# A decoder layer on one core: attention's eight PSUM banks dealt out by use instead of in mixed rings

## The chip, the cores and the metric

The kernel runs on one core of a Trainium2 chip. The metric is the device time of one execution in microseconds (us). The kernel before took 2240.39 us, the median of three runs (2234.24 to 2243.52).

## The reference

One decoder layer on 1040 positions (16 meta tokens and 1024 tokens) of width 1024, in float32:

```python
h = h + 0.5 * rms_norm(swiglu(rms_norm(h, g_ffn1_pre), w_ffn1_in, w_ffn1_out), g_ffn1_post)
u = rms_norm(h, g_mix_pre)
q, k, v, f_logit, c_b, c_c, c_in, gate_a, gate_c = split_cols(u @ w_in)
log_f = jax.nn.log_sigmoid(f_logit + b_forget)
y_attn = forgetting_attention(q, k, v, log_f) @ w_attn_branch   # softmax(q.k/8 + F[t] - F[s], causal) @ v
y_conv = (c_b * short_conv(c_c * c_in, conv_w)) @ w_conv_branch
mixed = (sigmoid(gate_a) * y_attn + sigmoid(gate_c) * y_conv) @ w_out
h = h + rms_norm(mixed, g_mix_post)
h = h + 0.5 * rms_norm(swiglu(rms_norm(h, g_ffn2_pre), w_ffn2_in, w_ffn2_out), g_ffn2_post)
```

Attention has 8 heads of 64 channels; F is the running sum of log_f.

## The kernel before, in words

Every float32 operand of a large product is split into a high and a low part, and a product is three matmuls (`mm3`, L142 to L146): high by high, low by high, high by low. The first feed-forward block, the projections, convolution and attention, the mixing, and the second feed-forward block follow each other. The stage that the change touches lies at about 740 to 1440 us of the span.

That stage goes like this. `values_in` (L728) projects the values of nine token blocks. Four passes (L828) compute the short convolution. Then a loop over 8 heads and 4 query pairs (L992 to L1009) runs attention. For each pair of heads `project_heads` (L901) multiplies out q and k, five pieces named `pqk`: two of q (512 columns each), three of k (264, 264, 512). ScalarE (L913) and VectorE (L914) drain each piece into one of two buffers `ha`, and SyncE copies it by DMA into `q` and `k` (L921, L923), four copies a piece. `softmax` (L925) multiplies scores into PSUM (`sc`, L937), one to three pieces for a query block; VectorE adds the forget bias and takes the minimum (L938), ScalarE the exponential (L942), VectorE the reciprocal and the scaling (L943, L944). `values` (L947) treats the query pair before: it transposes the weights, up to four 128x128 blocks into one bank (`tp`, L966), ScalarE and VectorE split the bank into two halves of a small buffer `hbc` (L139, L140; two places each, taken in turn), and two matmuls per key block (`pv`, L975 with the high half, L977 with the low) add into one output bank of 256 columns. ScalarE copies half of that bank out (L982), VectorE adds the other half (L983), the sum is split (L139, L140), and a DMA on ScalarE's queue stores it to `atd` (L986).

Between these dependent steps stands independent work: `fill_work` (L857) yields 32 gate projections (`pg`, 24 matmuls each) and then 16 products of the convolution branch (`pcb`, 12 matmuls each). Their results go into half pages (`tt`, L754) of a ring of four pages that the outputs of `values` use too, so that a gate result can wait for the store of an old attention output.

The order of the instructions on each engine is not the order of the code: a scheduler (`schedule_with_timeline_sim`) simulates the program with its own costs and takes, on each engine, the earliest instruction of the code that it thinks ready. What the engine gets is a fixed sequence, and an instruction whose input is late holds up everything behind it on its engine. The banks decide in it when a matmul may start: `Turns` (class in the code) deals out bank numbers in rotation, and the next user of a bank waits until the last one's result is read.

Before, `psO` deals banks 0 to 3 in one rotation to the scores and to the outputs, `psA` banks 4 and 5 to all projections and fill products, `psT` banks 6 and 7 to the transposed weights.

Of the kernel before, what the change touches and what calls it, by code (L numbers as in the profile page):

```python
# [49 lines left out]
class Split:  # L50
# [5 lines left out]
    def at(self, *sl):  # L56
        return Split(self.h[sl], self.l[sl])


def f32(ap):  # L60
    return ap.bitcast(F32)
# [6 lines left out]
def hybrid_layer(ctx, tc, x, meta, w_in, b_forget, conv_w, w_attn, w_conv, w_out,  # L68
# [69 lines left out]
    def split_into(h, l, src, eng=None):  # L138
        S.copy(h, src)  # L139
        (eng or V).tensor_sub(l, src, f32(h))  # L140
# [563 lines left out]
    def tH(tag, shape, name):  # L704

        turn[tag] += 1
        t = hbc[:, {"HB": 0, "HC": 2}[tag] + turn[tag] % 2]
        return t.rearrange("p a n -> p (a n)")[:, :shape[0] * shape[1]].rearrange("p (a n) -> p a n", a=shape[0])
# [38 lines left out]
        mix_input(1)  # L747


    psO, psA, psT = Turns(0, 1, 2, 3).bank, Turns(4, 5).bank, Turns(6, 7).bank  # L750
    loc = {"X": Turns(0, 1, 2, 3), "k": Turns(4, 5), "t": Turns(6, 7, 8, 9)}
    half_page = []

    def tt(n, name, dt=F32):  # L754

        if not half_page:
            t = loc["t"].page(name)
            half_page.extend((t[:, W0:W0 + H], t[:, :H]))
        t = half_page.pop()[:, :n]
        return t.bitcast(dt) if dt != F32 else t  # L760
# [185 lines left out]

    def values(h, qp, pr, v):  # L947

        po = psO(f"pv{h}_{qp}")[:, :256]
        first_mm = True  # L950
        vb, vm = v
        for s in range(2):
            V.tensor_copy(pmet[:, s, :META], pr[s][:, :META])
        for g in range(qp + 1, -1, -1):

            blks = [2 * g - 1, 2 * g] if g else [0]
            tp = psT(f"tp{h}_{qp}_{g}")

            at = lambda j, s: slice(256 * j + P * s, 256 * j + P * s + P)
            first_s = {2 * qp + 2: 1}  # L960
            hi = 0
            for j, b in enumerate(blks):
                k0 = META + P * (b - 1)
                for s in range(first_s.get(b, 0), 2):
                    c = at(j, s) if b <= 2 * qp + 1 else at(j, 0)
                    nc.tensor.transpose(tp[:, c], pr[s][:, k0:k0 + P] if b else pmet[:, s], ident)  # L966
                    hi = c.stop
            pth = tH("HB", [2, 256], f"pth{h}_{qp}_{g}").rearrange("p a b -> p (a b)")
            ptl = tH("HC", [2, 256], f"ptl{h}_{qp}_{g}").rearrange("p a b -> p (a b)")
            split_into(pth[:, :hi], ptl[:, :hi], tp[:, :hi])  # L970
            for j, b in enumerate(blks):
                vv = vb[:, b - 1, :] if b else vm
                s = first_s.get(b, 0)
                o, c = po[:, P * s:], slice(256 * j, 256 * j + 256 - P * s)
                mm(o, vv, pth[:, c], start=first_mm, stop=False)  # L975
                first_mm = False
                mm(o, vv, ptl[:, c], start=False, stop=b == 0)  # L977

        i = h % 2
        a, bo = DH * i, DH * (1 - i)  # L980
        os = tt(256, f"os{h}_{qp}")
        S.copy(os[a:a + DH], po[bo:bo + DH])  # L982
        V.tensor_add(os[a:a + DH], po[a:a + DH], os[a:a + DH])  # L983
        oh = tt(512, f"oh{h}_{qp}", F32R).rearrange("p (a b) -> p a b", a=2)
        split_into(oh[a:a + DH, 0], oh[a:a + DH, 1], os[a:a + DH])
        nc.scalar.dma_start(out=atd[:, a:a + DH, h // 2, qp * 256:qp * 256 + 256].rearrange("s p t -> p s t"),  # L986
                            in_=f32(oh[a:a + DH]))
# [4 lines left out]
    for h in range(NH):  # L992
        if h % 2 == 0:
            project_heads(h // 2)
        fb = fbuf[:, h % 2, :L]
        nc.sync.dma_start(out=fb, in_=fd[h:h + 1, :].broadcast_to([P, L]))
        v = (vbuf[:, h % 2], vmet[:, h % 2])
        load(f32(v[0]), vd[h, :, 1:, :])
        load(f32(v[1]), vd[h, :, 0, :])
        for qp in range(3, -1, -1):  # L1000
            pr = [softmax(h, 2 * qp + 1, fb), softmax(h, 2 * qp, fb)][::-1]
            if pend is not None:
                values(*pend)
            pend = (h, qp, pr, v)
            step += 1

            while done < (min(step * 32 // 25, 32) if step <= 25 else min(32 + (step - 25) * 16 // 7, 48)):
                next(fill)
                done += 1  # L1009
    values(*pend)  # L1010
    for _ in fill:
        pass

# [234 lines left out]
```

## Time and profile before

| | |
|---|---|
| profiled execution | 2236.28 us, span 2234.2 us, mean granted TensorE clock 0.978 |
| median of three timed runs | 2240.39 us |
| PE (matmul) busy | 2116.9 us, 95% of the span |
| DVE, ACT, POOL busy | 1434.0, 794.3, 140.5 us |
| chain that ended last | PE 80%, DMA 9%, DVE 7% |

PE is TensorE, DVE VectorE, ACT ScalarE, SP SyncE. A matmul's row gives a modelled length that overlaps the next one's: the distance from start to start, which the chain of waits prints, is what it takes of PE's time. The granted clock is 1.00 at 2.4 GHz and 0.50 at 1.2 GHz.

### The profile page before, as it was taken

To read this page: it belongs to the slowest core of one execution; us is meant where nothing else is said; L and a number is where in the kernel's file an instruction comes from. 1 tells how busy PE (TensorE), PEld (TensorE's weight loads), DVE (VectorE), ACT (ScalarE), POOL (GpSimd) and SP (SyncE) were. 2 spreads that over 40 slices of the span, in tenths; PEclk is the share of its full clock that TensorE was granted. 3 is DMA by queue.
4 is the path that set the end of the run, shared out by engine and by line. 5 is a ranking of instruction groups with operands and counts; after the bars stand their busy time and mean duration, and the time that the engine had idled before them with its cause. 6 is when DMAs were issued, how large, how long until landed. Compare 5 with 4: busy or idle time off the path is not lost.

```text
span 2234.2 us, 29992 instructions
## 1 busy us (share of the span) xinstructions
PE 2116.9 (95%) x11590; PEld 1835.9 (82%) x11590; DVE 1434.0 (64%) x2315; ACT 794.3 (36%) x1291; POOL 140.5 (6%) x181
## 2 busy tenths in 40 slices
PE   5899999999997999999999999899799999999996
PEld 5799999999886998888888787688588888878875
DVE  7976666655868643345454457656886666647788
ACT  6322222234234421134343344334432222224434
POOL 3000000000003200000010000012000000000000
PEclk9899999999999999999999999999899999999998
DMA  4322222368556542343434273833132222278574
GB/s 133 101 90 86 86 73 75 89 227 272 173 162 228 176 138 76 87 117 96 130 111 123 63 231 115 259 132 121 58 120 83 77 81 84 85 247 280 189 222 173
DMA packets 276967, 305.45 MB, mean 137 GB/s; under 512 B 12908, under 2 KB 184760, under 8 KB 276824
## 3 DMA queue, kind: packets, MB, share of 16 engines
q1 hardware_dynamic: 241072, 242.94, 35.8%
q10 hardware_dynamic: 35720, 60.59, 7.8%
q8 instruction: 91, 1.49, 0.3%
q14 instruction: 52, 0.43, 0.1%
q0 software_dynamic: 32, 0.00, 0.0%
HBM read 233.47 MB, written 57.36 MB: 130 GB/s over the span
## 4 chain that ended last, share of the span: by engine, by line
PE 80%; DMA 9%; DVE 7%; issue 2%; ACT 1%; SPq 1%; POOL 0%; ACTq 0%; POOLq 0%; DVEq 0%
PE wP L144 6%; PE wP L145 6%; PE wP L146 6%; PE vP L144 6%; PE vP L145 6%; PE vP L146 6%; PE pg L144 3%; PE pg L146 2%; PE pg L145 2%; PE 2P L145 2%; PE 2P L144 2%; PE 2P L146 2%; PE P L144 2%; PE P L145 2%; PE P L146 2%; DMA arP<-in_w_ffn_out_dram 2%
## 5 line engine op out<-in xcount | busy, mean ns | idle before, releaser
L145 PE MATMUL P<-blP,ahP 128*128 128x264 f32 (+1 forms) x452 | 144.7, 322 | 4.1 <-DVE ms_m0b L186 4.0
L144 PE MATMUL P<-bhP,ahP 128*128 128x264 f32 (+1 forms) x452 | 139.0, 324 | 8.4 <-ACT bhP L139 4.2
L146 PE MATMUL P<-bhP,alP 128*128 128x264 f32 (+1 forms) x452 | 143.8, 321 | 0.0
L145 PE MATMUL 2P<-lb2P,ha2P 128*128 128x512 f32 x264 | 103.8, 393 | 2.4 <-DVE lb2P L140 2.3
L146 PE MATMUL 2P<-hb2P,la2P 128*128 128x512 f32 x264 | 102.9, 391 | 0.0
L144 PE MATMUL 2P<-hb2P,ha2P 128*128 128x512 f32 x264 | 96.3, 394 | 2.8 <-ACT ha2P L139 2.4
L144 PEld LDWEIGHTS P<-bhP,ahP 128*128 128x128 f32 x452 | 85.7, 193 | 15.7 <-ACT bhP L139 5.2
L145 PEld LDWEIGHTS P<-blP,ahP 128*128 128x128 f32 x452 | 86.6, 192 | 10.4 <-DVE blP L140 4.9
L146 PEld LDWEIGHTS P<-bhP,alP 128*128 128x128 f32 x452 | 86.4, 191 | 5.7
L140 DVE TENSOR_TENSOR hbc<-tp,hbc 128x512 fp32r<-128x512 f32 (+2 forms) x112 | 62.8, 572 | 18.4 <-ACT hbc L139 17.3
L139 ACT CAST hbc<-tp 128x512 fp32r<-128x512 f32 (+2 forms) x112 | 52.8, 494 | 58.3 <-PE tp L966 55.6
L930 POOL TENSOR_TENSOR fbuf<-fbuf,rows 128x128 f32<-128x128 f32 x64 | 31.3, 489 | 576.5 <-DVE mn L938 481.9
L942 ACT ACTIVATE p<-p,mn 128x1040 f32<-128x1040 f32 (+3 forms) x64 | 50.6, 790 | 35.5 <-DVE mn L938 30.1
L145 PEld LDWEIGHTS 2P<-lb2P,ha2P 128*128 128x128 f32 x264 | 50.0, 189 | 14.5 <-DVE lb2P L140 4.1
L144 PEld LDWEIGHTS 2P<-hb2P,ha2P 128*128 128x128 f32 x264 | 49.7, 189 | 14.2 <-ACT ha2P L139 2.9
L937 PE MATMUL sc<-k,q 128*128 128x392 f32 (+6 forms) x224 | 54.7, 337 | 5.2 <-DVE mn L938 2.0
L146 PEld LDWEIGHTS 2P<-hb2P,la2P 128*128 128x128 f32 x264 | 49.9, 189 | 10.4
L938 DVE CUSTOM_DVE_ANT_0 p<-sc,fbuf 128x16 f32<-128x16 f32 (+3 forms) x64 | 28.5, 450 | 43.6 <-PE tp L966 30.5
L144 PE MATMUL pg<-um1h,g_h 128*128 128x512 f32 x128 | 51.4, 401 | 1.7 <-ACT oh L864 0.6
L144 PE MATMUL wP<-u1T2h,ws32h 128*128 128x264 f32 x176 | 50.9, 290 | 1.9 <-ACT u1T2h L139 1.2
L146 PE MATMUL wP<-u1T2h,ws32l 128*128 128x264 f32 x176 | 50.6, 289 | 2.0 <-DVE ws32l L140 2.0
L144 PE MATMUL pg<-um0h,g_h 128*128 128x512 f32 x128 | 50.8, 397 | 0.7 <-DVE ha L914 0.7
(795 smaller groups left out, 6914.9 us busy)
## 6 DMA issues: line engine op xcount, KB each, us to landing
arP<-in_w_ffn_out_dram SPq DMA_DIRECT2D x35, 512.0 KB
rb2P<-in_w_ffn_out_dram SPq DMA_DIRECT2D x35, 512.0 KB
ra2P<-g2d SPq DMA_DIRECT2D x30, 512.0 KB
wrb<-in_w_ffn_in_dram SPq DMA_DIRECT2D x22, 512.0 KB
vrb<-in_w_ffn_in_dram SPq DMA_DIRECT2D x22, 512.0 KB
g2d<-vuc ACTq DMA_DIRECT2D x44, 256.0 KB
brP<-g1d SPq DMA_DIRECT2D x20, 528.0 KB
wra<-in_w_ffn_in_dram SPq DMA_DIRECT2D x19, 512.0 KB
```

The lines of the kernel that those rows point to most:

```text
L139: S.copy(h, src)
L140: (eng or V).tensor_sub(l, src, f32(h))
L144: mm(o, a.h, b.h, start=start, stop=False)
L145: mm(o, a.h, b.l, start=False, stop=False)
L146: mm(o, a.l, b.h, start=False, stop=stop)
L930: G.tensor_add(fb[:, nk - P:nk], fb[:, nk - P:nk], mask)
L937: mm(sc[:, :ke - k0], q[:, s, qt * P:qt * P + P], k[:, k0:ke], start=s == 0, stop=s == 1)
L938: V.tensor_tensor_reduce(out=p[:, k0:k1], in0=sc[:, :k1 - k0], in1=fb[:, k0:k1], scale=1.0, scalar=mn[:, j - 1:j] if j else 3e38, op0=ALU. ...
L942: S.activation(p[:, :nk], p[:, :nk], AF.Exp, bias=low, scale=-1.0, accum_out=mn[:, 3:4])
```

## The change

From the convolution to the end of attention the banks are dealt out by use: banks 0 and 1 for scores (and for the last four blocks of `values_in`), 2 and 3 for projections and fill products, 5 to 7 for transposed weights, and bank 4 alone for the outputs of `values`. After attention the three old rotations are set up again.

```diff
-    psO, psA, psT = Turns(0, 1, 2, 3).bank, Turns(4, 5).bank, Turns(6, 7).bank
+    psO, psA, psT, psV = Turns(0, 1).bank, Turns(2, 3).bank, Turns(5, 6, 7).bank, Turns(4).bank
...
     def values(h, qp, pr, v):
 
-        po = psO(f"pv{h}_{qp}")[:, :256]
+        po = psV(f"pv{h}_{qp}")[:, :256]
...
     for _ in fill:
         pass
+
+    psO, psA, psT = Turns(0, 1, 2, 3).bank, Turns(4, 5).bank, Turns(6, 7).bank
```

No operation is added or taken away; PE has the same matmuls. The scheduler puts them in another order in this stage. Three places on PE show it.

First, the outputs of head 7, query pair 2. In the order before, two groups of transposes and their first output matmuls (`tp_2_2`, `tp_2_1`, then `pv_2`) stand back to back:

```order
L977 MATMUL pv_3_12601<-hbc,vmet 128x256
L966 MATMUL tp_2_2_12740<-ident,p_4_12587 128x128
L966 MATMUL tp_2_2_12740<-ident,p_5_12573 128x128
L966 MATMUL tp_2_2_12740<-ident,p_4_12587 128x128
L966 MATMUL tp_2_2_12740<-ident,p_5_12573 128x128
L966 MATMUL tp_2_1_12751<-ident,p_4_12587 128x128
L966 MATMUL tp_2_1_12751<-ident,p_5_12573 128x128
L966 MATMUL tp_2_1_12751<-ident,p_4_12587 128x128
L966 MATMUL tp_2_1_12751<-ident,p_5_12573 128x128
L975 MATMUL pv_2_12727<-hbc,vbuf 128x256
```

In the order now a score piece and two more groups stand between `tp_2_1` and `pv_2`, and `tp_2_2` has moved ahead of a whole fill product:

```order
L966 MATMUL tp_2_1_12751<-ident,p_4_12587 128x128
L966 MATMUL tp_2_1_12751<-ident,p_5_12573 128x128
L966 MATMUL tp_2_1_12751<-ident,p_4_12587 128x128
L966 MATMUL tp_2_1_12751<-ident,p_5_12573 128x128
L937 MATMUL sc_0_0_12831<-k_1_11818,q_1_11817 128x256 x2
L966 MATMUL tp_2_0_12762<-ident,pmet 128x128 x2
L966 MATMUL tp_1_2_12841<-ident,p_2_12717 128x128
L966 MATMUL tp_1_2_12841<-ident,p_3_12703 128x128 x2
L975 MATMUL pv_2_12727<-hbc,vbuf 128x256
```

So the transposes have moved away from the matmuls that read them.

Second, on PE, the scores of head 5 right behind the outputs of head 4 (`pv_0`). Before, six score pieces crowd behind one output, each in a bank that an output or a score has just left:

```order
L975 MATMUL pv_0_11412<-hbc,vmet 128x256
L937 MATMUL sc_6_0_11401<-k_1_10782,q_1_10781 128x456 x2
L977 MATMUL pv_0_11412<-hbc,vmet 128x256
L937 MATMUL sc_5_1_11472<-k_1_10782,q_1_10781 128x392 x2
L937 MATMUL sc_4_1_11486<-k_1_10782,q_1_10781 128x328 x2
L937 MATMUL sc_4_0_11482<-k_1_10782,q_1_10781 128x328 x2
L937 MATMUL sc_3_0_11610<-k_1_10782,q_1_10781 128x264 x2
L937 MATMUL sc_3_1_11614<-k_1_10782,q_1_10781 128x264 x2
L144 MATMUL pg_512_11691<-um1h_7280,g_h 128x512
```

Now there are output matmuls between the first pieces, and a gate projection follows the third:

```order
L937 MATMUL sc_6_0_11401<-k_1_10782,q_1_10781 128x456 x2
L977 MATMUL pv_1_11300<-hbc,vbuf 128x256
L975 MATMUL pv_1_11300<-hbc,vbuf 128x256
L977 MATMUL pv_1_11300<-hbc,vbuf 128x256
L966 MATMUL tp_0_0_11425<-ident,pmet 128x128 x2
L975 MATMUL pv_1_11300<-hbc,vmet 128x256
L937 MATMUL sc_6_1_11405<-k_1_10782,q_1_10781 128x456 x2
L977 MATMUL pv_1_11300<-hbc,vmet 128x256
L937 MATMUL sc_5_0_11468<-k_1_10782,q_1_10781 128x392 x2
L144 MATMUL pg_0_11580<-um0h_6271,g_h 128x512
```

The crowd has been spread over the gate projections.

Third, on PE, the first scores of the last pair of heads, which read k fresh from its DMA. Before, after `sc_7_0` come five transposes and a long run of gate matmuls (`sc_7_1` stands 35 of them later):

```order
L937 MATMUL sc_7_0_11980<-k_0_11816,q_0_11815 128x16 x2
L966 MATMUL tp_0_1_12012<-ident,p_0_11729 128x128
L966 MATMUL tp_0_1_12012<-ident,p_1_11719 128x128 x2
L966 MATMUL tp_0_0_12022<-ident,pmet 128x128 x2
L144 MATMUL pg_0_12035<-um0h_6271,g_h 128x512
```

Now only six output matmuls and two gate matmuls stand between:

```order
L937 MATMUL sc_7_0_11980<-k_0_11816,q_0_11815 128x16 x2
L975 MATMUL pv_0_12009<-hbc,vbuf 128x256
L977 MATMUL pv_0_12009<-hbc,vbuf 128x256
L975 MATMUL pv_0_12009<-hbc,vbuf 128x128
L977 MATMUL pv_0_12009<-hbc,vbuf 128x128
L975 MATMUL pv_0_12009<-hbc,vmet 128x256
L977 MATMUL pv_0_12009<-hbc,vmet 128x256
L144 MATMUL pg_0_12035<-um0h_6271,g_h 128x512
L145 MATMUL pg_0_12035<-um0l_6273,g_h 128x512
L937 MATMUL sc_7_1_11984<-k_0_11816,q_0_11815 128x512 x2
```

The second score has moved towards the copies of k.

## Rows read from the trace of the kernel before

**Rows 1.** Busy time by stretch: stretch, length, busy of engines, clock, DMA, GB/s.

```profile
966.00:1078.00 112.00, 109.81 (x599) 93.78 (x597) 57.41 (x158) 47.54 (x98) 7.50 (x16) 1.00 0.38 104
1078.00:1192.00 114.00, 110.65 (x601) 94.21 (x600) 58.94 (x160) 46.87 (x98) 8.72 (x16) 1.00 0.43 117
1192.00:1309.00 117.00, 111.13 (x592) 94.26 (x593) 57.41 (x158) 45.49 (x96) 7.51 (x16) 0.99 0.34 96
1309.00:1410.00 101.00, 92.80 (x496) 77.71 (x494) 69.91 (x187) 46.54 (x101) 6.67 (x14) 0.98 0.57 177
1410.00:1425.00 15.00, 8.82 (x27) 6.58 (x27) 3.49 (x8) 2.46 (x5) 0.00 (x0) 0.66 0.97 330
```

**Rows 2.** Who PE waited for, 966 to 1425: total us, times, longest us.

```profile
PE pab L145 <- DMA ab1l<-atd: 3.4, 1, 3.4
PE pv L977 <- DVE hbc L140: 3.3, 7, 0.6
...
PE pqk L144 <- ACT oh L864: 2.1, 1, 2.1
PE pv L975 <- ACT hbc L139: 2.0, 3, 1.1
PE sc L937 <- DVE mn L938: 2.0, 3, 0.8
...
PE sc L937 <- DVE os L983: 1.5, 2, 0.8
PE sc L937 <- DMA k<-ha: 1.4, 2, 1.2
...
PE tp L966 <- DVE hbc L140: 1.0, 1, 1.0
...
PE pg L144 <- ACT oh L864: 0.6, 1, 0.6
PE pg L144 <- ACT gt L864: 0.6, 1, 0.6
PE pqk L144 <- ACT gt L864: 0.6, 1, 0.6
```

**Rows 3.** Chain of waits, two pieces: start us, us from start to start.

```profile
986.34 0.76 PE tp L966 x7
...
1253.20 0.12 PE pv L975
1253.32 0.23 PE pg L146
```

**Rows 4.** Groups by line, splitting of transposed weights: busy us, mean ns, idle before.

```profile
L140 DVE TENSOR_TENSOR hbc<-tp,hbc 128x512 fp32r<-128x512 f32 (+2 forms) x112 | 62.8, 572 | 18.4 <-ACT hbc L139 17.3
L139 ACT CAST hbc<-tp 128x512 fp32r<-128x512 f32 (+2 forms) x112 | 52.8, 494 | 58.3 <-PE tp L966 55.6 <-DVE hbc L140 1.0 <-issue 0.5
```

**Rows 5.** Timeline by engine, 1252 to 1264: start, us, instruction, idle before.

```profile
1257.86 0.65 PE L937 MATMUL sc<-k,q 128*128 128x456 f32 x2 [0.72 <-DVE os L983]
1258.66 0.37 ACT L982 COPY gt<-pv 64x256 f32<-64x256 f32 x1 [0.51 <-PE pv L977]
1259.59 0.41 DVE L983 TENSOR_TENSOR gt<-pv,gt 64x256 f32<-64x256 f32 x1
```

**Rows 6.** Timeline by engine at the first scores, 940 to 975.

```profile
966.37 0.36 PE L937 MATMUL sc<-k,q 128*128 128x16 f32 x2
970.21 1.03 PE L937 MATMUL sc<-k,q 128*128 128x512 f32 x4
966.41 0.43 DVE L914 SCALAR_TENSOR_TENSOR ha<-pqk,ha 128x264 fp32r<-128x264 f32 x1 [7.30 <-ACT ha L913]
```

**Rows 7.** Groups by line: the softmax of one query block.

```profile
L938 DVE CUSTOM_DVE_ANT_0 p<-sc,fbuf,mn 128x512 f32<-128x512 f32 (+4 forms) x48 | 30.7, 640 | 20.8 <-PE sc L937 17.4 <-POOL fbuf L930 2.5 <-issue 0.3
L942 ACT ACTIVATE p<-p,mn 128x1040 f32<-128x1040 f32 (+3 forms) x64 | 50.6, 790 | 35.5 <-DVE mn L938 30.1 <-DVE mn L943 4.1
L944 DVE TENSOR_SCALAR p<-p,mn 128x1040 f32<-128x1040 f32 (+3 forms) x64 | 35.8, 562 | 1.8
```

## The prediction

> **What bounds the kernel now.** I read the busy time by stretch first. In the four stretches that hold attention, 966 to 1410 us, PE is busy for all but 2.2, 3.4, 5.9 and 8.2 us (length less busy time), 19.6 us in all [rows 1]. So PE sets the pace, the change takes no matmul from it, and what it can win is what PE loses between matmuls in these 444 us. The list of waits comes second and says what these 19.6 us are [rows 2]. I sort them by what the banks can do to them.
>
> A. Transposed weights: `pv` and `tp` waiting for the split into `hbc`: 3.3 + 2.0 + 1.0 = 6.3 us, 11 times.
> B. Scores waiting for a bank that another score or an output still holds (`sc` for `mn` L938 and `os` L983): 2.0 + 1.5 = 3.5 us, 5 times.
> C. Projections waiting for a gate result (`oh` and `gt`, L864): 2.1 + 0.6 + 0.6 + 0.6 = 3.9 us, 4 times. ScalarE can't write it, because the half page is still to be stored from an older attention output.
> D. Scores waiting for k: 1.4 us.
>
> What is left of the 19.6 are waits for `ha` and for loads, which I leave as they are. Behind attention PE loses another 6.2 us of 15 (15.00 less 8.82) before the attention branch's product, since that waits for a load of the stored outputs [rows 1, 2].
>
> The third view is the chain of waits, for what a matmul takes from start to start: 0.23 us for 512 columns, 0.12 for 256, 0.76/7 = 0.11 for a transpose [rows 3]. With these I price the work that stands on PE between two instructions in the order of before and of the change. It is no forecast of a time, only how much cover each wait has, and it is how the terms below are scaled: a measured wait, times cover missing now over cover missing before.
>
> **The change part by part.**
>
> Three banks for transposed weights (A). A transpose's result is ready for the high matmul after ScalarE's 0.494 us, for the low one after VectorE's 0.572 more [rows 4]; with about 0.1 for handing over I ask 0.6 and 1.2 us of cover. The order of before falls below 1.2 us to the high matmul in 22 of the 112 groups, the order now in 2. That is not all the cover that counts: `hbc` still has only two places, so a split also waits until the output matmuls two groups back have read theirs. With both conditions the missing cover sums to 5.7 us before and 1.7 now. 6.3 x 1.7/5.7 = 1.9, so A wins 4.4 us. The bounds: 6.3 if all of it goes, 0 if the two places of `hbc` decide.
>
> Two banks for scores, one for outputs (B). A score's bank is read in 0.64 us on VectorE [rows 7]. An output's bank is read by ScalarE from 1258.66 and by VectorE until 1259.59 + 0.41 = 1260.00, which is 1.34 us [rows 5]. Asking 0.85 and 1.3, the order before lacks cover at 13 handovers, 7.0 us together; the order now at 8, 3.7 us together. The crowd of six score pieces of head 5, one of whose waits is the 0.72 us in [rows 5], is spread out. 3.5 x 3.7/7.0 = 1.8: B wins 1.7 us, between 3.5 and a loss that is the first rival below.
>
> Gate results (C). Places where a projection comes less than 5 us of cover behind the last output matmul whose store frees its half page: six before, three now. I take off a third: 1.3 us, between 0 and 3.9.
>
> Copies of k (D), a new cost. With fewer banks in the mixed ring, the scheduler brings the second score of a head pair (`sc_7_1`) forward. In the second, third and fourth pair it now stands 1.9, 2.1 and 1.2 us of work behind the first score. It reads keys 16 to 527, whose second piece is drained at about the moment of the first score: at the first pair the drain starts at 966.41, the first score at 966.37, and the second score starts at 970.21 without a wait [rows 6]. So the copy arrives no later than 3.8 us after the drain's start, and no earlier than the drain itself (0.43). With 3.8 the three waits sum to 1.9 + 1.7 + 2.6 = 6.2 us, with 0.43 to nothing; I take the upper middle, 3.6, since four DMAs must be issued for each piece. Against that, the first score of the third pair now has some 2 us more cover behind its q, which pays back 1.2 of the 1.4 us of D. Behind the waiting score stand the gate matmuls, so PE stands still for all of it. Net loss 2.4.
>
> Later softmax. Scores come later, so their weights come later before the transposes: the least cover from the last score to the first transpose falls from 4.2 us to 2.2 and 2.3, in two places. The path is 0.64 + 0.79 + 0.56 = 2.0 us at mean sizes [rows 7], plus handing over and what VectorE has in front. I take 1 us at each of the two: loss 2, between 0 and 4.
>
> Clock and restarts. The granted clock is 0.99 over 117 us and 0.98 over 101 [rows 1], which is 1.2 + 2.0 = 3.2 us of work lost; after waits of several us it has fallen towards the half level (0.66 in the last stretch). Fewer waits give back 1 us (0 to 3.2). A row shows a wait only past the modelled end of the matmul before; some 12 fewer waits at the 0.16 us that it so hides (estimate: about 0.28 us of row length against 0.12 from start to start) give 2 more.
>
> What stays. The wait at 1410 stays: it begins with the drain of head 7's second-to-last outputs, and both orders put about 8 us of PE work behind that. Before 966 PE is taken as covered in both orders; 24 matmuls of the first convolution product only move into the end of the mixing block. Price of being wrong there: about 1 us either way. After attention the orders agree, and the shift goes through to the end.
>
> Sum: -4.4 - 1.7 - 1.3 + 2.4 + 2.0 - 1.0 - 2.0 = -6.0 us. The profiled execution took 2236.28, so 2230.3; its time lies 4.1 below the median of the three runs, so for a median I predict 2240.4 - 6.0 = 2234.
>
> **A rule that speaks against it.** The Trainium skill says in "Perfetto Trace Analysis", section "Optimizing Tensor Performance", that independent matmul groups should go round different PSUM banks, so that draining one overlaps the next group's matmuls. The 31 handovers from one output to the next no longer do that. By that rule, with nothing else between, 31 drains of 1.34 us would be added, 42 us, and the sum would come to 2276. The trace of before can't show a ring of one; what it shows is one score waiting 0.72 us for an output's bank [rows 5], and the sum above counts the cover instead. The mechanism is weighed as the first rival.
>
> **Rivals.**
>
> 1. The single output bank (slower). Place: the 31 handovers from one output to the next. For it: the readers of that bank stand in ScalarE's and VectorE's queues behind other work, and everything on PE stands behind the next `pv`. Against it: in the order now only 3 handovers have under 1.3 us of other PE work between. If the drain takes 3 us, the missing cover is 11 us; 4 us, 19; 5 us, 31. With 4 us: -6 + 19 = +13, 2253. It eats the gain from 2.2 us on (5.9 missing there) and costs 0.5% from 3.9. For a drain to be that long the queues would have to be three times as late as in [rows 5].
>
> 2. The waits change place (no change). k's copies cost their upper bound, 6.2 - 1.2 = 5.0, and softmax 4: -4.4 - 1.7 - 1.3 - 3.0 + 9.0 = -1.4 us, 2239. For it: both new costs are bounded only by rows that show no wait there. Against it: the copies would have to need the whole 3.8 us. That the rotation hardly touches PE's waits, because `hbc` with two places decides instead, ends here too.
>
> 3. All of it goes. A, B, C and D vanish with the clock's loss and the restarts: 6.3 + 3.5 + 3.9 + 1.4 + 3.2 + 2.0 = 20 us, 2220. For it: missing cover for the transposes is nearly gone in the order. Against it: C and D hang on DMAs that the banks don't touch.
>
> **How the numbers follow.** Forecast 0.48, its own range 2228 to 2238 (the bounds of the softmax and k terms); no change 0.28; all gone 0.12; slower 0.12. Differences below 0.5%, 11 us, are about what a measurement of this kernel can't tell from none. Faster by more: all of rival 3 and a fifth of the forecast's share, 0.22. Slower by more: rival 1 and a little of rival 2, 0.14. Within: 0.64. The range reaches past rival 3's 2220 and to just short of rival 1's 2253: 2217 to 2251.
>
> **What would show it.** In the list of waits of the new profile, `pv` and `tp` for `hbc` should fall from 6.3 us to about 2, and `sc` for `mn` and `os` from 3.5 to about 2, with nothing left near head 5's crowd. `sc` for k should rise from 1.4 to about 4, at the second to fourth pair. A line of `tp` waiting for VectorE's scaling (L944) should be new. The wait for `ab1l` should stay at 3 to 4 us. I am wrong if `pv` waits for L982 or L983 by more than 2 us in sum (rival 1), if the idle time in attention stays near 19 us (rival 2), or if the time changes outside attention.

## The result and the profile after

The changed kernel takes 2225.43 us, median of five runs (2223.51 to 2226.51), beside 2235.96 (2234.24 to 2243.52) for the kernel before: ratio 0.9947 with the 95% interval 0.9934 to 0.9960. The medians lie 10.5 us apart (0.47%), and the interval, 0.40 to 0.66% of the time before, is 8.9 to 14.8 us. So the gain is clear of nothing and above the 6.0 that were forecast, but the interval doesn't tell on which side it lies of the 0.5% that the prediction called no change. The span of the profiled execution falls from 2234.2 to 2223.3 us, by 10.9.

Busy time by stretch of the kernel after, the same five stretches as [rows 1]:

```profile
966.00:1078.00 112.00, 110.49 (x607) 95.17 (x608) 57.87 (x158) 48.40 (x99) 8.52 (x16) 1.00 0.38 105
1078.00:1192.00 114.00, 111.78 (x610) 94.96 (x609) 61.37 (x167) 48.88 (x100) 7.62 (x16) 1.00 0.46 124
1192.00:1309.00 117.00, 114.69 (x620) 98.19 (x619) 57.01 (x161) 46.42 (x99) 8.92 (x16) 0.99 0.38 112
1309.00:1410.00 101.00, 89.28 (x456) 73.69 (x456) 65.01 (x178) 43.34 (x95) 7.63 (x14) 0.93 0.58 182
1410.00:1425.00 15.00, 15.00 (x66) 12.16 (x66) 10.88 (x18) 5.26 (x9) 0.00 (x0) 0.99 0.92 307
```

PE loses 1.5, 2.2, 2.3 and 11.7 us instead of 2.2, 3.4, 5.9 and 8.2. The last two stretches aren't the same work in both kernels, since the program has slid forward under the fixed times: the end wait that stood behind 1410 now stands before it. So the stretch to compare runs from the first score of attention to the first product of the attention branch (`pab`), before and then after:

```profile
966.37:1412.82 446.45, 424.06 (x2282) 359.90 (x2281) 244.56 (x664) 186.82 (x393) 30.39 (x62) 0.99 0.43 123
```

```profile
965.30:1401.67 436.37, 422.36 (x2281) 359.26 (x2281) 240.99 (x663) 187.34 (x391) 32.68 (x62) 0.99 0.44 126
```

The stretch is 10.1 us shorter, and 8.4 of them are PE's idle time (446.45 - 424.06 = 22.4 against 14.0). Another 1.1 us stands ahead of it. No shorter wait of PE between 740 and 950 us accounts for it; what is shorter are waits ahead of 740 us, where the code is the same (`wP` for `u1B11l` 5.2 us before, 4.0 after), so it can't be put down to the banks. Behind the stretch nothing changes much.

Who PE waited for, 950 to 1425, in the kernel after (total us, times, longest), to be laid beside [rows 2]:

```profile
PE pab L145 <- DMA ab1l<-atd: 3.9, 1, 3.9
PE pv L975 <- DVE gc L983: 2.8, 2, 1.9
PE sc L937 <- DMA k<-ha: 2.6, 4, 1.7
PE pv L977 <- DVE hbc L140: 1.6, 4, 0.5
PE pcb L144 <- DVE cp L886: 1.5, 3, 0.6
PE sc L937 <- DVE mn L938: 1.5, 5, 0.5
PE pg L144 <- ACT gt L864: 1.4, 1, 1.4
PE tp L966 <- DVE p L944: 0.9, 1, 0.9
PE pab L144 <- DMA ab1h<-atd: 0.5, 1, 0.5
PE tp L966 <- DVE pmet L953: 0.3, 1, 0.3
PE pv L975 <- ACT hbc L139: 0.3, 1, 0.3
PE pg L144 <- DVE ha L914: 0.2, 1, 0.2
```

`pab` is the product of the attention branch, `ab1h` and `ab1l` are its loads of the stored outputs, and `gc`, `gt`, `ga`, `os` and `oh` are names that the trace gives to half pages of the one ring, so that `gc` from L983 is an output. The sum is 17.5 us, 25.1 before. The waits for `hbc` (A) are 1.9 us. No score waits for an output (`os`) any more. Two things are new: an output waits for the output before it (`gc`, L983), and a transpose for the scaled weights (`p`, L944).

The split of the transposed weights, by line, shows what replaced the bank (mean ns; idle before, and what ended it):

```profile
L140 DVE TENSOR_TENSOR hbc<-tp,hbc 128x512 fp32r<-128x512 f32 (+2 forms) x112 | 62.8, 571 | 60.8 <-ACT hbc L139 46.8
L139 ACT CAST hbc<-tp 128x512 fp32r<-128x512 f32 (+2 forms) x112 | 53.3, 494 | 55.3 <-PE pv L975 42.3
```

In [rows 4] ScalarE's split waited for the transposes, 55.6 of 58.3 us. Now it waits for `pv`, 42.3 of 55.3: the transposes lie ready in their third bank, and the two places of `hbc` decide when a split may start. The durations are the same.

The price of the single output bank, in the timeline by engine at the last output (start, us, instruction, idle before):

```profile
1398.79 0.36 ACT L982 COPY gc<-pv 64x256 f32<-64x256 f32 x1
1399.31 0.42 DVE L140 TENSOR_TENSOR hbc<-tp,hbc 128x256 fp32r<-128x256 f32 x1
1399.76 0.43 DVE L983 TENSOR_TENSOR gc<-pv,gc 64x256 f32<-64x256 f32 x1
1400.24 0.39 PE L975 MATMUL pv<-hbc,vbuf 128*128 128x256 f32 x1 [1.94 <-DVE gc L983]
```

The bank is read from 1398.79 to 1400.19, 1.40 us, because VectorE puts a split first; [rows 5] had 1.34. Both are single readings: over all 32 outputs, from the start of L982 to the end of L983 in the timeline, a bank is read for 0.82 to 2.54 us, 1.32 on average, and in the kernel before for 0.82 to 2.37, 1.13 on average. Both waits of an output stand where no fill product lies between it and the output before, the other at 1383.75 (0.86 us, behind a reading of 1.87 us).

### The profile page after: what moved, and what is told of

Same layout as the page of the kernel before. It is cut to its first block, busy times and chain, and to the rows that moved or that the text cites. A ratio compares the mean times of both kernels' runs of the same rounds, so it can differ in the third digit from the quotient of the medians.

```text
span 2223.3 us, 30057 instructions
## 1 busy us (share of the span) xinstructions
PE 2117.7 (95%) x11590; PEld 1837.0 (83%) x11590; DVE 1430.4 (64%) x2315; ACT 794.5 (36%) x1291; POOL 141.3 (6%) x181
## 4 chain that ended last, share of the span: by engine, by line
PE 78%; DMA 9%; DVE 8%; issue 2%; ACT 2%; SPq 1%; POOL 0%; ACTq 0%; POOLq 0%; DVEq 0%
PE wP L144 6%; PE wP L145 6%; PE wP L146 6%; PE vP L144 6%; PE vP L145 6%; PE vP L146 6%; PE pg L144 2%; PE pg L145 2%; PE pg L146 2%; PE P L144 2%; PE P L145 2%; PE P L146 2%; PE 2P L145 2%; PE 2P L144 2%; PE 2P L146 2%
## 5 line engine op out<-in xcount | busy, mean ns | idle before, releaser
L139 ACT CAST hbc<-tp 128x512 fp32r<-128x512 f32 (+2 forms) x112 | 53.3, 494 | 55.3 <-PE pv L975 42.3
L145 PEld LDWEIGHTS 2P<-lb2P,ha2P 128*128 128x128 f32 x264 | 49.8, 189 | 15.4 <-DVE lb2P L140 5.1
L937 PE MATMUL sc<-k,q 128*128 128x264 f32 (+6 forms) x224 | 57.6, 340 | 4.4 <-DMA k<-ha 2.6
L139 ACT CAST ws14h<-ws 128x1024 fp32r<-128x1024 f32 x22 | 23.2, 1054 | 79.8 <-PE wP L145 63.0
L145 PE MATMUL wP<-u1T2l,ws32h 128*128 128x264 f32 x176 | 51.2, 291 | 0.3 <-DVE u1T2l L140 0.3
```

Of the source, the lines that this page charges most:

```text
L145: mm(o, a.h, b.l, start=False, stop=False)
L937: mm(sc[:, :ke - k0], q[:, s, qt * P:qt * P + P], k[:, k0:ke], start=s == 0, stop=s == 1)
```

## The experiments

All rings are one line. In the changed kernel it is the line of the diff above, with `psO` for scores, `psA` for projections, `psT` for transposed weights, `psV` for outputs. Each ring experiment replaces that line alone; the scheduler then makes its own order.

**renum**: the old sharing under the new numbers.

```diff
+    psO, psA, psT = Turns(0, 1, 4, 5).bank, Turns(2, 3).bank, Turns(6, 7).bank; psV = psO
```

> The banks as before (four in one ring for scores and outputs, two for projections, two for transposed weights), but with the change's numbers for projections (banks 2 and 3); PE's order in attention is that of before. Theory (the order of PE's instructions decides, not which banks are which): within 2 us of before, about 2235. Rival (the other bank numbers, or the projections that start earlier before attention, are the gain): near 2226.

Measured: 2238.09 us, ratio 1.0004 (0.9991 to 1.0016); `hbc` waits 6.3 us as before. Which numbers the banks have, and the setting up of new rings after attention, cost and bring nothing.

**third_t**: a third bank for transposed weights, outputs still among the scores.

```diff
+    psO, psA, psT = Turns(0, 1, 4).bank, Turns(2, 3).bank, Turns(5, 6, 7).bank; psV = psO
```

> A third bank for transposed weights alone: scores and outputs stay in one ring, now of three banks. Cover missing on PE by the order: transposes 1.3 us (before 8.4, change 1.7), scores and outputs 6.9 (before 7.0, change 3.7). Theory (the room for transposed weights pays most): two thirds of the gain or more, 2226 to 2229. Rival (taking outputs and scores apart pays): no gain, 2234 to 2237.

Measured: 2228.16 us, 0.9961 (0.9945 to 0.9977). Its list of waits:

```profile
PE sc L937 <- DVE os L983: 3.6, 3, 2.1
PE tp L966 <- DVE p L944: 3.1, 3, 1.7
PE pv L975 <- DVE mn L938: 2.6, 3, 0.9
...
PE pv L977 <- DVE hbc L140: 0.7, 3, 0.4
```

With the third bank `hbc` falls from 6.3 to 0.7 us (seven_mixed, below, shows that the shorter mixed ring by itself leaves it at 6.3). In the mixed ring of three, scores wait for outputs (3.6) and outputs for scores (2.6).

**own_v**: outputs apart, the eighth bank to scores.

```diff
+    psO, psA, psT, psV = Turns(0, 1, 5).bank, Turns(2, 3).bank, Turns(6, 7).bank, Turns(4).bank
```

> Outputs in a bank of their own, scores in three, transposed weights in two as before. Cover missing: transposes 5.1 us (before 8.4), scores and outputs 3.5 (before 7.0). Theory (room for transposed weights pays): a third of the gain, 2231 to 2234. Rival (taking apart pays): nearly all of it, 2225 to 2228.

Measured: 2229.53 us, 0.9962 (0.9948 to 0.9976), with `hbc` waits of 4.1 us (listed in the slowest of its nine runs). The time is between what the theory and its rival expected, and most of the gain is there without the third bank for transposed weights.

**two_v**: the eighth bank to outputs.

```diff
+    psO, psA, psT, psV = Turns(0, 1).bank, Turns(2, 3).bank, Turns(6, 7).bank, Turns(4, 5).bank
```

> The change with one bank moved from transposed weights (now two) to outputs (now two). Cover missing: transposes 9.7 us, scores 1.2, outputs 0. Theory: the gain is lost, 2234 to 2238. Rival (taking apart pays, the single output bank costs): as fast as the change or faster, 2222 to 2227.

Measured: 2235.92 us, 0.9996 (0.9985 to 1.0007): nothing is left of the gain. Its list of waits has no `pv` for L983 any more, and 6.7 us for `hbc`:

```profile
PE pv L977 <- DVE hbc L140: 3.4, 9, 0.8
PE pv L975 <- ACT hbc L139: 3.3, 7, 0.9
```

Two output banks take away the waits that one has, 2.8 us, and buy no time: idle_bank below, with the same rings and one output bank, comes to 0.9993. The rule of the Trainium skill that the prediction weighed ("Perfetto Trace Analysis", section "Optimizing Tensor Performance": groups should go round several banks) doesn't decide here: 31 handovers cost two waits, and not 42 us.

**idle_bank**: as the changed kernel, bank 5 unused.

```diff
+    psO, psA, psT, psV = Turns(0, 1).bank, Turns(2, 3).bank, Turns(6, 7).bank, Turns(4).bank
```

> The change with bank 5 unused: scores two, outputs one, projections two, transposed weights two, seven banks in all. Cover missing: transposes 6.1 us (before 8.4, change 1.7), scores and outputs 3.0 (before 7.0, change 3.7). Theory (total missing cover sets the gain: 15.4 before gave 0, 8.2 and 8.6 gave 8 to 9 us, 5.4 gave 12): 9.1 missing, so about 7 us under before, 0.996 to 0.998, and two fifths of the change's gain belong to the third transpose bank. Rival (the third transpose bank is what pays, taking apart alone does nothing): 0.999 to 1.001.

Measured: 2235.61 us, 0.9993 (0.9981 to 1.0005). Parts of its list:

```profile
PE pg L144 <- ACT gt L864: 5.9, 3, 3.0
...
PE pv L977 <- DVE hbc L140: 2.3, 7, 0.5
...
PE pv L975 <- DVE gc L983: 2.1, 2, 1.7
...
PE pv L975 <- ACT hbc L139: 0.7, 1, 0.7
```

Taking the uses apart gives nothing with seven banks, so the theory that missing cover by itself sets the gain (0.996 to 0.998) failed here. `hbc` is down to 3.0 us all the same, and gate projections wait 5.9 us instead, with 2.2 more at `pqk` (all gate results 8.1, before 3.9): the waits changed places. Between this run and the changed kernel lies one bank, and 0.46%.

**third_a**: outputs apart, the eighth bank to projections.

```diff
+    psO, psA, psT, psV = Turns(0, 1).bank, Turns(2, 3, 5).bank, Turns(6, 7).bank, Turns(4).bank
```

> The change with bank 5 given to projections and fill products (three) instead of transposed weights (two). Cover missing: transposes 4.3 us, scores and outputs 3.7, 8.0 in all. Theory (total missing cover): 8 to 9 us under before, ratio 0.995 to 0.997. Rival (where the eighth bank goes matters: only transposed weights can use it): like the kernel with bank 5 unused, or slower by the gate results that then wait in more banks, 0.998 to 1.001.

Measured: 2227.10 us, 0.9955 (0.9939 to 0.9971).

```profile
PE pab L145 <- DMA ab1l<-atd: 4.0, 1, 4.0
PE pab L144 <- DMA ab1h<-atd: 3.9, 1, 3.9
PE pv L977 <- DVE hbc L140: 3.3, 4, 1.9
PE pv L975 <- ACT hbc L139: 2.3, 4, 1.0
...
PE pg L144 <- ACT gt L864: 1.0, 1, 1.0
```

With 0.6 more at `tp`, `hbc` stands at 6.2 us, as before the change, and yet the time is that of the changed kernel within the intervals. So the waits for `hbc` aren't the only ones whose end can pay.

**mixed_a**: the third bank for projections, outputs among the scores.

```diff
+    psO, psA, psT = Turns(0, 1, 4).bank, Turns(2, 3, 5).bank, Turns(6, 7).bank; psV = psO
```

> Scores and outputs share three banks (0, 1, 4) in one ring, projections get three (2, 3, 5), transposed weights two (6, 7): nothing is taken apart by use and the transposes keep before's two banks. If before simply had one bank too many in the mixed ring, and any other use can make something of it, this gains like the runs with a third bank for transposes: ratio to before 0.995 to 0.997, waits of PE for hbc near 6 us but waits for gate results (gt, oh, L864) under 1.5 us against before's 3.3. If the gain needs the third transposed-weights bank, or the outputs apart from the scores, the ratio is 0.999 to 1.001.

Measured: 2235.52 us, 1.0002 (0.9993 to 1.0012). The gate waits did fall, to 1.8 us (under 1.5 was expected), and the time didn't. In the profiled execution, 3 us above the median of its runs, the end of attention has longer waits instead:

```profile
PE pab L145 <- DMA ab1l<-atd: 4.5, 1, 4.5
PE pab L144 <- DMA ab1h<-atd: 3.7, 1, 3.7
PE pcb L145 <- DMA cb1l<-cvd: 3.2, 1, 3.2
PE pcb L144 <- DVE cp L886: 3.1, 2, 1.6
```

**seven_mixed**: before's sharing with the mixed ring one bank shorter.

```diff
+    psO, psA, psT = Turns(0, 1, 4).bank, Turns(2, 3).bank, Turns(6, 7).bank; psV = psO
```

> Seven banks: scores and outputs share a ring of three (0, 1, 4), projections 2 and 3, transposed weights 6 and 7; bank 5 holds nothing. If the mixed ring of four had a bank to spare, the time stays: ratio to before 0.999 to 1.001, sum of PE's waits from 950 to 1425 some 25 us as before; then third_t's gain is wholly the third bank for transposed weights and not the shorter mixed ring. If the mixed ring needs its fourth bank, this is slower, 1.002 to 1.005, with more waits of scores for outputs (sc for os, L983, over 3 us), and the third bank for transposed weights is worth the more. If it is 0.996 to 0.998, the shorter ring by itself gives the scheduler a better order.

Measured: 2233.27 us, 0.9982 (0.9971 to 0.9994), between the bands expected; `hbc` 6.3 us, all waits 23.1. The fourth bank of the mixed ring wasn't needed: without it the kernel is no slower, rather 0.2% faster. From here to third_t a third bank for transposed weights brings another 0.2%, with intervals that just overlap; from idle_bank to the changed kernel it brings 0.46%, with intervals that lie apart.

Together (the eighth bank's use, the ratio with outputs among the scores, and with outputs apart):

| eighth bank | among | apart |
|---|---|---|
| scores | 1.0004 | 0.9962 |
| projections | 1.0002 | 0.9955 |
| transposed weights | 0.9961 | 0.9947 |
| outputs | the row of scores | 0.9996 |
| none | 0.9982 | 0.9993 |

The expectations count the cover that each order lacks. In that count the versions stand as in their ratios (5.4, 8.0, 8.2, 8.6, 9.1 and 10.9 us for 0.9947, 0.9955, 0.9961, 0.9962, 0.9993 and 0.9996, and 15.4 for the kernel before), though the intervals of neighbours overlap and the steps aren't in proportion: from 8.6 to 9.1 us it is 0.3%, from 9.1 to 15.4 next to nothing.

**ab_split** and **ab_split_before**: the load of the stored outputs, for which `pab` waits behind attention, cut in four per half, in the changed kernel and in the kernel before.

```diff
-        for s, t in enumerate((ab.h, ab.l)):
-            nc.scalar.dma_start(out=f32(t), in_=atd[s, :, :, half * H:half * H + H])
+        for k in range(4):
+            for s, t in enumerate((ab.h, ab.l)):
+                nc.scalar.dma_start(out=f32(t[:, k]), in_=atd[s, :, k, half * H:half * H + H])
```

> The change, with the load of the stored attention outputs cut into four, one per pair of heads, so that only the last pair's piece hangs on the last stores. PE's order up to the branch product is the change's. Theory (the wait at the end of attention is the length of one load behind the last drain, and the changed order only shifts it): PE's 4.4 us of waits for ab1h and ab1l fall below 1.5, and with the clock kept up the time is 4 to 7 us under the change, 2219 to 2222. Rival (the wait is for the last stores themselves, or twelve more DMAs on ScalarE's queue hold up its casts): within 2 us of the change, 2224 to 2228.

> The same cut of the load in the kernel before, with its banks. Theory (the end wait is independent of the banks): 6.2 us of waits fall below 1.5, 5 to 9 us under before, 2229 to 2233, and the change on top keeps its gain of some 8 to 12 us between these two runs. Rival (part of the change's gain came only from a shorter end wait): the two runs of the cut load lie 6 us or less apart.

Measured: 2221.82 us, 0.9929 (0.9915 to 0.9943), and 2232.89 us, 0.9981 (0.9968 to 0.9994). The chain of waits of the changed kernel shows what is cut: the last store into this half leads to one load of all four head pairs, and that to `pab` (start, us from start to start):

```profile
1392.50 3.42 DMA atd<-oh
...
1396.62 9.85 DMA ab1l<-atd
...
1406.52 0.80 PE pab L145
```

`pab` needs the last head pair only in its fourth step, so 9.85 us of load for all of them is too much to wait for. In ab_split no wait for `ab1` is listed, and the next input, `ga`, makes PE wait 1.2 us. In ab_split_before no wait for `ab1` is listed either, but the wait isn't gone:

```profile
PE pab L144 <- DVE ga L1030: 6.6, 1, 6.6
```

In this execution the cut moved the wait to `ga`; under 1.5 us had been expected. It is the slowest of the twelve, 2239.91 us, 7 above their median, so the others may have less of it. ScalarE's own list there has a split of an output (`oh`, L139) held up for 2.9 us behind a piece of the cut load (`ab0l`), as the rival in ab_split's expectation had it; whether that makes `ga` late isn't shown. By the times the banks are worth the same on top of the cut: 0.9929/0.9981 = 0.9948, against 0.9947 without.

**ab_split_a**: the cut and the third bank for projections.

```diff
+    psO, psA, psT, psV = Turns(0, 1).bank, Turns(2, 3, 5).bank, Turns(6, 7).bank, Turns(4).bank
```

> The changed kernel with the load of the stored outputs cut in four per half (as in ab_split), and bank 5 given to projections instead of to transposed weights (as in third_a). If the two gains add, as they did for ab_split: ratio to before 0.992 to 0.9945, PE waits no longer for ab1l. If third_a's own wait for that load (7.9 us in two pieces, the largest seen) was all lost time, the cut is worth more here than the 3.6 us it gave the changed kernel: 0.990 to 0.992, some 2217 us, and this would be the best version. If the cut only moves the wait, 0.9955.

Measured: 2215.96 us, 0.9912 (0.9893 to 0.9932), the best version here, though its interval overlaps ab_split's. In its list 0.4 us of third_a's 7.9 is left, and the next input is late:

```profile
PE pab L144 <- DVE ga L1032: 3.3, 1, 3.3
...
PE pab L145 <- DMA ab1l<-atd: 0.4, 1, 0.4
```

## Why the prediction was right, and where not

The direction was right and the time lies in the range of 2217 to 2251, but below the forecast's own 2228 to 2238. The gain was forecast at 6.0 us and is 10.9 between the profiled spans. Term by term, by the lists of waits (one execution each):

| term | forecast | measured |
|---|---|---|
| A, `hbc` | -4.4 | 6.3 to 1.9: -4.4 |
| B, scores (3.5, and 0.2 for `gt` of L983), with `pv` for L983 | -1.7 | 3.7 to 1.5, and +2.8: +0.6 |
| C, gate results | -1.3 | 3.9 to 1.4: -2.5 |
| D, k | +2.4 | 1.4 to 2.6: +1.2 |
| later softmax | +2.0 | `p` and `pmet`: +1.2 |
| what stays: `ab1` | 0 | 6.2 to 4.4: -1.8 |
| what stays: `ha` | 0 | 2.0 to 0.2: -1.8 |
| what stays: before 966 | 0 | -1.1 |
| clock and restarts | -3.0 | the rest: -2.2 (and 0.1 at `cp`) |

**The step that failed is "What stays", with the waits for `ha` that the opening left as they are.** These three rows make 4.7 of the 4.9 us that the forecast lacks. The other errors cancel by luck: B came out 2.3 us worse and the clock term 0.7, C, D and the softmax 1.2, 1.2 and 0.8 better.

Of the three only `ha` is seen to be a gain of the new order: gate projections hardly wait any more for the projection bank that a q or k piece still holds (0.2 us left). The 1.1 us before 966 can't be put down to the banks, as said above. And the 1.8 us at `ab1` are mostly time that PE lost sooner. The wait begins with the drain of head 7's second output of four (the prediction calls it second-to-last). From there to `pab`, before and then after:

```profile
1398.26 0.36 ACT L982 COPY gc<-pv 64x256 f32<-64x256 f32 x1
1412.82 1.22 PE L144 MATMUL pab<-ab1h,wab_h 128*128 128x512 f32 x2 [2.79 <-DMA ab1h<-atd]
```

```profile
1388.24 0.36 ACT L982 COPY gc<-pv 64x256 f32<-64x256 f32 x1
1401.67 0.96 PE L144 MATMUL pab<-ab1h,wab_h 128*128 128x512 f32 x2 [0.46 <-DMA ab1h<-atd]
```

PE was ready for `pab` 11.8 us behind that drain (1412.82 - 2.79 - 1398.26) and is now 13.0, since some of the products between run at a low clock (below). The load itself takes 9.85 us in the chain, where the chain of before has

```profile
1406.57 10.80 DMA ab1l<-atd
```

So the three rows say where the forecast and the spans differ, but beyond the 1.8 us of `ha` it stays open how much of the 4.7 the banks brought. With the load cut, the gain was the same within some 0.2%, which can't confirm 1.8 us either, the less since ab_split_before has a wait of 6.6 us in its place.

**A** had mechanism and size in the list of waits: third_t shows the third bank taking the `hbc` waits away, and the L139 row that the places of `hbc` take over. The size has some luck in it, since the expectations count the missing cover of before as 8.4 us where the prediction has 5.7; with 8.4, A would be 5.0. What the forecast didn't see is that A isn't needed for a gain of this size (third_a, `hbc` 6.2 us). A list of waits says what an order loses, not what another order would lose.

**B and rival 1.** The mark set for rival 1, more than 2 us of `pv` for L983, was reached: 2.8. Its price wasn't. The longest of 32 drains took 2.54 us and their mean is 1.32, where the rival needed 3.9, and two_v beside idle_bank shows that a second output bank is worth nothing.

**D.** With 3.6 us for a copy the waits for k at the second, third and fourth pair of heads would be 1.7, 1.5 and 2.4 us; the list has 2.1, 0.3 and none there, and 0.2 at the first.

**Rival 2**, waits that change places, is what idle_bank and two_v did. The forecast kernel escaped it by giving the bank to the transposes.

**Clock and restarts.** One microsecond of clock was to come back; nothing did. Length times missing clock over the five stretches is 8.3 us in [rows 1] (1.2 + 2.0 + 5.1) and 8.4 after (1.2 + 7.1 + 0.15). Besides the end wait there is a dip inside attention, before and then after:

```profile
1375.00:1380.00 5.00, 3.15 (x10) 2.20 (x10) 4.07 (x13) 2.60 (x5) 0.91 (x2) 0.74 0.43 125
1380.00:1385.00 5.00, 4.94 (x27) 4.08 (x26) 3.81 (x11) 2.58 (x5) 0.46 (x1) 0.92 0.21 60
```

```profile
1385.00:1390.00 5.00, 3.93 (x15) 3.15 (x16) 3.36 (x11) 2.19 (x6) 0.00 (x0) 0.64 0.58 172
1390.00:1395.00 5.00, 5.00 (x23) 4.09 (x22) 2.21 (x4) 1.39 (x3) 0.00 (x0) 0.68 0.38 115
```

It costs 5 x (0.26 + 0.08) = 1.7 us before and 5 x (0.36 + 0.32) = 3.4 after. What the end wait costs fell from 5.1 us to some 3.5 (5 x 0.16 + 5 x 0.50 from 1400 to 1410, and 0.15), so the two changes cancel. The lists hold 32 waits before and 25 after, 7 fewer and not 12; whether restarts make up the rest of 2.2 us isn't shown.

**The level.** 2234 was set from a median of three; five runs put the kernel before 4.4 us lower, at 2235.96 (2234.5 to 2238.4 in the sessions of the experiments). About half of the 8.6 us between 2234 and 2225.43 is that, the other half the gain.

What stays open: why taking the outputs apart is worth 0.4% with the eighth bank at scores (renum to own_v) or projections (mixed_a to third_a) and nothing with seven banks (seven_mixed to idle_bank). Each line gives another order, and no wait common to the three pairs was found. One execution's list doesn't explain it all either: third_a's waits sum to 23.2 us, hardly under the 25.1 before, with the changed kernel's time. Third places for `hbc`, which the L139 row suggests, weren't tried.

## What to carry to other kernels

Where a scheduler orders the work, a bank's use is judged by all the waits of the new order, not by the wait that it was meant for: with the outputs apart the same spare bank gave 0.3 to 0.5% over leaving it unused at three uses and nothing at the fourth, and with the outputs among the scores it paid at one use alone. Before giving a resource to the loudest wait, leave it unused for one run and move it through the other uses. And look for the one load behind the last store of a stage: cutting it was worth another 0.2% here, and 0.4% in a version that waited longer for it (third_a to ab_split_a).

## What the runs showed of the hardware

- A bank that two engines read one after the other is taken for 0.82 to 2.54 us (32 outputs of the changed kernel, 1.32 on average), though the reads take 0.37 and 0.41 to 0.43; the rest is the second engine's queue. Even so 29 of the 31 handovers in a ring of one show no wait on PE.
- After the wait of 3.90 us at the end of attention, `pab`'s 512-column matmuls run 0.43 us from start to start, against 0.23 in [rows 3]; the clock granted from 1405 to 1410 is 0.50, the half level. The clock granted over the stretch 1309 to 1410 is 0.93, lower than before's 0.98, in the faster kernel: a stretch's clock can't be compared when waits have slid into it.
- Five runs of each kernel told 0.53% from nothing with an interval of 0.13% either side, finer than the 0.5% that the prediction had allowed.
